# The first mixer's convolution by eight token phases with one fp32 product each, and the heads' query-key part emitted apart

## Chip, cores and metric

The kernel runs on one core of one Trainium2 chip. The metric is the device time of one execution in microseconds (us); the kernel before takes 2222.93 us (median of 3 runs, 2222.47 to 2223.78).

## The reference

A decoder trunk of two layers on x of 1024 tokens by 1024 channels, float32. Each layer is a mixer and a SwiGLU block (hidden width 2816), each with an RMS norm before it and a residual sum; a last RMS norm closes. The change is in the first layer's mixer, cut to what matters:

```python
ca, cg, q, k, v, og, gates = split(h @ w_in)       # 512 channels each, gates 8
u = ca * sigmoid(cg)
u = causal_depthwise_conv(u, conv_w, conv_b)       # 31 taps, 512 channels
u = silu(layernorm(u, ln_g, ln_b))                 # over the 512 channels
qk = silu(causal_depthwise_conv(concat(q, k), ...))  # 4 taps
hm = mlstm(q, k, v, gates)                         # 4 heads of 128
hm = head_rmsnorm(hm * sigmoid(og))
return concat(u, hm) @ w_out
```

The mLSTM works in chunks: scores of query and key with a decay, a state carried from chunk to chunk, and a stabiliser.

## The kernel before

Everything is kept channel by token, 128 channels on the partitions; tokens come in two halves of 512. Large products run in three passes (`mm3`, lines 142 to 144): every fp32 operand is split into a rounded part and the rest (a ScalarE copy and a VectorE subtraction: `split`, lines 126 and 127; for weights lines 137 and 138), and high times low, low times high and high times high are summed in PSUM. Weights come by a DMA (line 134) into one of two staging tiles `raw`, and their parts go to the tiles `wH` and `wL`, three buffers each. Small products (scores L513, transposes L517, state L536 to L539, means L348) are single fp32 products.

`mixer0` goes through the list `ORDER0`. `c` is `conv_in` for 128 channels: two projections, the gate, and a store of u by token phase to DRAM (L313, L316). `v` is `conv`, `l` the layer norm, `g` a head's value and output gate, `q` its query and key (`head_qk`), `x` its `head_mix` (a letter a or b after the number means one half), `n` a head norm, `k` the preparation of the output projection's right side (`cut`), which reads layer-norm tiles back (`conv_out`, L386) and finishes heads (`head_out`). The list gives the order of emission. A scheduler that simulates the program decides each engine's own order; `high_priority(offset)` pulls an instruction ahead.

The convolution folds the token axis into PH = 4 phases: a tile has 32 channels times 4 phases on the partitions, and NT = 256 steps of 4 tokens along the free axis. The 31 taps become SH + 1 = 9 band matrices of 128 by 128 (the first half empty), one for each shift. For each of 16 channel groups `conv` loads the bands (544 KB), splits them, loads the group's u from DRAM (L332), splits it to `uH` and `uL` (L126, L127), and runs 9 x 3 products of 256 columns into half a PSUM bank; ScalarE adds the bias on the way out (L339). `layer_norm` takes mean and variance with products by `ones_p` (L348), normalises, applies the affine and silu in 16 pairs of activations and a combine (L376 to L378), and stores by phase to `zd` (L380). `head_mix` first loads two rows (L507, L508), forms scores (L513) and transposed keys (L517), masks, takes exponentials (L519, L522), then runs the chunk products and the state (L536 to L558).

The output projection's weights come through the same tiles; for half 0 the fourth block of them uses the mixer's `u` tiles instead (`spare`, named `uw` in the trace).

Of the kernel before, what the change touches and what calls it, by code (L numbers as in the profile page):

```python
# [12 lines left out]
ALU = mybir.AluOpType  # L13
# [9 lines left out]
PH = 4  # L23
CG = 32
NT = T // PH
SH = 8
# [3 lines left out]
ORDER0 = ['c0', 'g0', 'c1', 'c2', 'q0', 'v0', 'c3', 'x0a', 'v1', 'x0b', 'g1', 'v2', 'q1', 'v3', 'x1', 'l', 'g2', 'q2', 'q3', 'x2a', 'g3', 'x3a', 'x2b', 'n3', 'k0', 'n1a', 'x3b', 'n1b']  # L30
CUT0 = (range(7), range(7, 8))
UB = 4
# [14 lines left out]
KB = 1  # L47
# [17 lines left out]
    0, 16, 32, 40, 56, 72, 88, 120, 128, 132, 136, 144)  # L65
# [3 lines left out]
def trunk_kernel(ctx, tc, xT, cols, gate_b0, ev_vo0, ev_u, ev_cw, ev_out, od_v0, od_u, od_out, gate_w2,  # L69
# [13 lines left out]
    def nm(s):  # L83
        uid[0] += 1
        return f"{s}_{uid[0]}"
# [23 lines left out]
    hln = cp.tile([P, 32], F32, tag="hln", name="hln")  # L109
    DVE.tensor_scalar(out=hln, in0=col[:, C_LG:C_LG + 32], scalar1=0.5, scalar2=None, op0=ALU.mult)  # L110
# [3 lines left out]
    def c1(i):  # L114
        return col[:, i:i + 1]
# [123 lines left out]
    def spare(src, mp):  # L239

        with tc.high_priority(offset=OOFF):
            raw = wp.tile([P, 1088], F32, tag="raw", name=nm("raw"), bufs=2)[:, :1024]
            SP.dma_start(raw, src)
            parts = []
            for c in range(2):
                hi, low = (mp.tile([P, HALF + 30], F32R, tag="u", name=nm("uw"), bufs=UB)[:, :HALF] for _ in range(2))
                split((hi, low), raw[:, c * HALF:(c + 1) * HALF], DVE)
                parts.append((hi, low))
        return parts


    def mixer0(cut, then):
        with tc.tile_pool(name="m0", bufs=1, reuse_waits="tile") as mp:
# [47 lines left out]
            def conv_in(i):  # L301

                wa = nextw(DVE)
                wg = nextw(DVE)
                for half in range(2):
                    u = mp.tile([P, HALF], F32, tag="u", name=nm("u"), bufs=UB)
# [6 lines left out]
                    DVE.scalar_tensor_tensor(out=u.rearrange("c (s n) -> c n s", s=PH), in0=g.rearrange("c (n s) -> c n s", s=PH),  # L313
                                             scalar=0.5, in1=rr[half].rearrange("c (n s) -> c n s", s=PH),
                                             op0=ALU.mult, op1=ALU.mult)
                    SP.dma_start(ud[i][:, :, half * P:(half + 1) * P], u.rearrange("c (s n) -> c s n", s=PH))  # L316

            def conv(i):


                for j in range(2):
                    b = bank("sm")
                    y = xy(2 * i + j if i < 2 else 2 * i + j - 4, int(i > 1))
                    Y.append(y)
                    for e in range(2):
                        g = 4 * i + 2 * j + e
                        w = weights(ev_cw[g], 1088, DVE)
                        c0 = (2 * j + e) * CG
                        with tc.high_priority(offset=WOFF):
                            raw = mp.tile([P, NT + SH], F32, tag="ur", name=nm("ur"), bufs=GB)  # L330
                            DVE.memset(raw[:, :SH], 0.0)
                            SP.dma_start(raw[:, SH:], ud[i][c0:c0 + CG].rearrange("c s n -> (c s) n"))  # L332
                            d = tuple(mp.tile([P, NT + SH], F32R, tag=t, name=nm(t), bufs=GB) for t in ("uH", "uL"))
# [9 lines left out]
            def by_phase(t):  # L343
                return t.rearrange("p (e n) -> p e n", e=2)

            def mean(b, s):
                for e in range(2):
                    PE.matmul(b, ones_p, s[:, e * NT:(e + 1) * NT], start=e == 0, stop=e == 1)  # L348

            def layer_norm():  # L350

                s = tp.tile([P, HALF], F32, tag="s", name=nm("s"), bufs=1)
                DVE.tensor_tensor(out=s, in0=Y[0], in1=Y[1], op=ALU.add)
                for y in Y[2:]:
                    DVE.tensor_tensor(out=s, in0=s, in1=y, op=ALU.add)
                mu = bank("sm")[:, :NT]
                mean(mu, s)
                s = tp.tile([P, HALF], F32, tag="s", name=nm("s"), bufs=1)
                for j, y in enumerate(Y):
                    DVE.tensor_tensor(out=by_phase(y), in0=by_phase(y), in1=mu.unsqueeze(1).to_broadcast([P, 2, NT]),  # L360
                                      op=ALU.subtract)
                    t = tmp() if j else s
                    ACT.activation(t, y, AF.Square)
                    if j:
                        DVE.tensor_tensor(out=s, in0=s, in1=t, op=ALU.add)
                var = bank("sm")[:, :NT]
                mean(var, s)
                r = tp.tile([P, HALF], F32, tag="r", name=nm("r"), bufs=1)[:, :NT]
                rsqrt(r, var)
                for j, y in enumerate(Y):  # L370
                    DVE.tensor_tensor(out=by_phase(y), in0=by_phase(y), in1=r.unsqueeze(1).to_broadcast([P, 2, NT]), op=ALU.mult)
                    t = tmp()
                    for e in range(2):
                        g = 2 * j + e
                        sl = slice(e * NT, (e + 1) * NT)
                        ACT.activation(t[:, sl], y[:, sl], AF.Tanh, bias=hln[:, 16 + g:17 + g], scale=hln[:, g:g + 1])  # L376
                        ACT.activation(y[:, sl], y[:, sl], AF.Identity, bias=hln[:, 16 + g:17 + g], scale=hln[:, g:g + 1])
                    DVE.scalar_tensor_tensor(out=y, in0=t, scalar=1.0, in1=y, op0=ALU.add, op1=ALU.mult)  # L378
                    for e in range(2):
                        SP.dma_start(zd[2 * j + e].rearrange("c a n -> a c n"), y[:, e * NT:(e + 1) * NT])  # L380

            def conv_out(k, half, d):

                z = xy(k, half)
                with tc.high_priority(offset=WOFF):
                    SP.dma_start(z.rearrange("c (a n) -> c a n", a=PH),  # L386
                                 zd[4 * k:4 * k + 4, :, :, half * P:(half + 1) * P].rearrange("g c a n -> (g c) a n"))
                z = z.rearrange("c (a n) -> c n a", a=PH)
                split(tuple(t.rearrange("c (n a) -> c n a", a=PH) for t in d), z, DVE)
# [113 lines left out]
            def head_mix(hd, half, q, k, v, og, st):  # L503
# [5 lines left out]
                cc, wk, em = gcols["c"], gcols["wk"], gcols["em"]  # L509
# [10 lines left out]
                for c in range(4):  # L520
# [7 lines left out]
                                  in1=wk[:, half * 4:half * 4 + 4, hd:hd + 1].to_broadcast([P, 4, P]), op=ALU.mult)  # L528
                for c2 in range(2):
# [57 lines left out]
            for what in ORDER0:  # L587
# [17 lines left out]
                elif what[0] == "x":  # L605
                    for half in halves:
                        heads[n]["s"] = head_mix(n, half, heads[n][0, half], heads[n][1, half], heads[n]["v"],
                                                 heads[n]["o"], heads[n]["s"] if half else None)
# [627 lines left out]
def _layout(i):  # L1236
# [22 lines left out]

    cw = i["ev_conv_w"][0].reshape(TAPS, 16, CG)  # L1260
    band = np.zeros((16, CG, PH, SH + 1, PH, CG), np.float32)
    for c in range(CG):
        for m in range(SH + 1):
            for sp in range(PH):
                for ap in range(PH):
                    j = 4 * (m - SH) + sp - ap + TAPS - 1
                    if 0 <= j < TAPS:
                        band[:, c, sp, m, ap, c] = cw[j, :, c]
    band = band.reshape(16, P, SH + 1, P)
    assert not band[:, :, 0, 64:].any()  # L1270
    band = cat([band[:, :, 1:].reshape(16, P, SH * P), band[:, :, 0, :64]], axis=2)
    qw = i["ev_qk_conv_w"][0].reshape(4, 8, P).transpose(2, 1, 0).reshape(P, 32)
    cols = cat([colv(i["mix_norm_g"]), colv(i["ffn_norm_g"]), colv(i["final_norm_g"]),
                phased(i["ev_conv_b"][0]), phased(i["ev_ln_g"][0]), phased(i["ev_ln_b"][0]), qw, colv(i["ev_qk_conv_b"]), colv(i["ev_head_g"]),
# [57 lines left out]
def _build(a):  # L1332
# [10 lines left out]
    args.append(nc.dram_tensor("zd", (16, CG, PH, NT), F32, kind="Internal").ap())  # L1343
# [15 lines left out]
```

## Time and profile before

| | before |
|---|---|
| median of 3 runs | 2222.93 us |
| profiled execution | 2222.86 us |
| its span, first to last instruction | 2221.1 us |
| TensorE products busy | 2181.1 us (98%) |
| VectorE busy | 1624.6 us (73%) |
| ScalarE busy | 899.2 us (40%) |
| mean granted TensorE clock | 0.995 |

The time of the execution is 1.8 us more than the span. TensorE's products are pipelined: a record's duration is longer than its distance to the next one, so what a product costs in a row of products is read from start to start. The granted clock is a share of 2.4 GHz; 0.5 is 1.2 GHz.

### The profile page before, as it was taken

The page shows a single profiled execution, that of the slowest core. Times are in us where ns is not written, and L with a number is a line of the kernel's source. Part 1 is how long each engine was busy: PE and PEld are TensorE (multiplying, and loading weights), DVE is VectorE, ACT ScalarE, POOL GpSimd, SP SyncE. Part 2 cuts the span into 40 slices and gives each one's busy share as a digit, 9 for nine tenths or more (in the row PEclk, how much of TensorE's full clock was granted, in tenths as well). Part 3 has the DMA queues.
Part 4 walks back from the last instruction along what each step waited for, and adds up shares of the span by engine and source line. Part 5 has one row for each costly group of instructions (what it writes and reads, how often), then busy time and mean ns, then how long its engine had stood idle before and what let it go on. Part 6 is the DMA issues. An engine that isn't in the chain of part 4 may idle for free.

```text
span 2221.1 us, 29368 instructions
## 1 busy us (share of the span) xinstructions
PE 2181.1 (98%) x10956; PEld 1851.6 (83%) x10956; DVE 1624.6 (73%) x2721; ACT 899.2 (40%) x1489; POOL 18.2 (1%) x56
## 2 busy tenths in 40 slices
PE   8999999899999999999999999999999999999997
PEld 6889899788888888888788989888788888888887
DVE  6564688669887677877867566677788877678686
ACT  5223364445222222444555444554432222234553
POOL 0000000000000000000020000000000000000000
PEclk9999999999999999999999999999999999999999
DMA  4233425536443324735421111044454423275343
GB/s 163 73 94 98 122 75 159 180 128 200 169 152 104 110 100 139 270 105 148 137 68 39 39 39 39 29 127 165 156 195 169 141 87 119 95 246 164 97 123 125
DMA packets 130719, 276.90 MB, mean 125 GB/s; under 512 B 13808, under 2 KB 31088, under 8 KB 130576
## 3 DMA queue, kind: packets, MB, share of 16 engines
q1 hardware_dynamic: 129424, 273.97, 37.9%
q8 instruction: 86, 1.41, 0.3%
q10 hardware_dynamic: 1152, 1.05, 0.1%
q14 instruction: 57, 0.47, 0.1%
HBM read 208.35 MB, written 66.62 MB: 124 GB/s over the span
## 4 chain that ended last, share of the span: by engine, by line
PE 92%; DVE 5%; ACT 1%; DMA 1%; issue 1%; DVEq 0%; SPq 0%; ACTq 0%
PE mm L142 20%; PE mm L143 20%; PE mm L144 20%; PE sm L142 9%; PE sm L143 9%; PE sm L144 9%; PE sm L775 1%; DVE xy L882 1%; PE sm L792 1%; PE sm L793 1%; PE sm L795 1%; DVE wL L138 0%; DVE xy L1227 0%; DMA raw<-in_ev_u 0%; DVE hL L127 0%
## 5 line engine op out<-in xcount | busy, mean ns | idle before, releaser
L143 PE MATMUL mm<-hL,wH 128*128 128x512 f32 x1420 | 558.0, 393 | 0.6 <-DVE hL L279 0.6
L144 PE MATMUL mm<-hH,wH 128*128 128x512 f32 x1420 | 557.4, 393 | 0.0
L142 PE MATMUL mm<-hH,wL 128*128 128x512 f32 x1420 | 525.5, 395 | 17.3 <-DVE wL L138 11.6
L142 PEld LDWEIGHTS mm<-hH,wL 128*128 128x128 f32 x1420 | 267.5, 189 | 74.9 <-ACT s L169 7.7
L143 PEld LDWEIGHTS mm<-hL,wH 128*128 128x128 f32 x1420 | 267.8, 189 | 57.0 <-DVE hL L279 2.1
L144 PEld LDWEIGHTS mm<-hH,wH 128*128 128x128 f32 x1420 | 267.8, 189 | 55.0
L143 PE MATMUL sm<-hL,wH 128*128 128x512 f32 x616 | 240.8, 391 | 0.0
L144 PE MATMUL sm<-hH,wH 128*128 128x512 f32 x616 | 239.9, 390 | 0.0
L142 PE MATMUL sm<-hH,wL 128*128 128x512 f32 x616 | 209.7, 391 | 0.6 <-DVE wL L127 0.5
L126 ACT ACTIVATE wH<-S 128x1024 fp32r<-128x1024 f32 x88 | 93.3, 1060 | 224.9 <-PE sm L144 223.2
L979 DVE TENSOR_TENSOR c<-sm,c 128x512 f32<-128x512 f32 x144 | 97.4, 689 | 113.4 <-PE sm L144 98.3
L126 ACT ACTIVATE wH<-q 128x512 fp32r<-128x512 f32 x143 | 90.4, 632 | 183.8 <-PE mm L144 104.3
L138 DVE TENSOR_TENSOR wL<-raw,wH 128x1024 fp32r<-128x1024 f32 (+2 forms) x95 | 117.5, 1236 | 61.1 <-ACT wH L137 61.0
L137 ACT ACTIVATE wH<-raw 128x1024 fp32r<-128x1024 f32 (+2 forms) x95 | 101.5, 1068 | 149.8 <-PE mm L144 96.3
L127 DVE TENSOR_TENSOR wL<-q,wH 128x512 fp32r<-128x512 f32 x143 | 98.9, 691 | 69.1 <-ACT wH L126 68.8
L142 PE MATMUL mm<-wH,hL 128*128 128x256 f32 (+2 forms) x512 | 144.5, 288 | 2.6 <-DVE t L310 1.9
L143 PE MATMUL mm<-wL,hH 128*128 128x256 f32 (+2 forms) x512 | 146.5, 288 | 0.0
L144 PE MATMUL mm<-wH,hH 128*128 128x256 f32 (+2 forms) x512 | 146.4, 288 | 0.0
L142 PEld LDWEIGHTS sm<-hH,wL 128*128 128x128 f32 x616 | 115.4, 188 | 25.6 <-DVE wL L127 0.7
L143 PEld LDWEIGHTS sm<-hL,wH 128*128 128x128 f32 x616 | 115.7, 188 | 25.3 <-issue 1.0
L126 ACT ACTIVATE wH<-raw 128x1024 fp32r<-128x1024 f32 x66 | 70.0, 1061 | 164.6 <-PE sm L144 130.4
L144 PEld LDWEIGHTS sm<-hH,wH 128*128 128x128 f32 x616 | 115.7, 188 | 24.3 <-issue 0.5
(302 smaller groups left out, 3941.0 us busy)
## 6 DMA issues: line engine op xcount, KB each, us to landing
raw<-in_w SPq DMA_DIRECT2D x108, 512.0 KB
mdT<-c SPq DMA_DIRECT2D x88, 256.0 KB
m<-mdT SPq DMA_DIRECT2D x88, 256.0 KB
mdB<-c SPq DMA_DIRECT2D x66, 256.0 KB
q<-in_w SPq DMA_DIRECT2D x60, 256.0 KB
m<-mdB SPq DMA_DIRECT2D x55, 256.0 KB
xsp<-xy SPq DMA_DIRECT2D x48, 256.0 KB
raw<-in_ev_u SPq DMA_DIRECT2D x22, 512.0 KB
```

What stands on the lines that cost most here:

```text
L126: ACT.activation(dst[0], src, AF.Copy)
L127: lo.tensor_tensor(out=dst[1], in0=src, in1=dst[0], op=ALU.subtract)
L137: ACT.activation(hi, raw, AF.Copy)
L138: lo.tensor_tensor(out=low, in0=raw, in1=hi, op=ALU.subtract)
L142: PE.matmul(o, lt[1], rt[0], start=start, stop=False)
L143: PE.matmul(o, lt[0], rt[1], start=False, stop=False)
L144: PE.matmul(o, lt[0], rt[0], start=False, stop=stop)
L775: PE.matmul(lb[:, j * P:(j + 1) * P], X[:, 2 * j * P:(2 * j + 1) * P], X[:, (2 * j + 1) * P:(2 * j + 2) * P], start=True, stop=True)
L792: PE.matmul(db[:, cc, :], kw[:, cs], v[:, c, :], start=True, stop=True)
L793: PE.matmul(ob[:, cc, :], A[:, cs], v[:, c, :], start=True, stop=st is None)
L795: PE.matmul(ob[:, cc, :], qt[:, cs], st, start=False, stop=True)
L979: DVE.tensor_tensor(out=out, in0=a, in1=b, op=ALU.add)
```

## The change

The convolution has 8 phases, 16 channels in a group, 32 groups, and 128 steps along the free axis; 5 full band matrices per group (320 KB), each with one fp32 product instead of three. Nothing is split: bands go by DMA into `wH` and `wL` in turn, data into one tile for four groups. The bias is added by VectorE for four groups at once. The affine and silu leave the layer norm for `conv_out`, behind the read from `zd`, where channels lie on the partitions. u is stored once for both halves. `head_mix` is cut in two, `head_pre` (row loads, scores, transposes, exponentials, scaled query and key) and the rest; `ORDER0` has `a` entries that emit `head_pre` earlier. The layout on the host and the constant columns follow.

```diff
-PH = 4
-CG = 32
-SH = 8
+PH = 8
+CG = 16
+SH = 4
-ORDER0 = ['c0', 'g0', 'c1', 'c2', 'q0', 'v0', 'c3', 'x0a', 'v1', 'x0b', 'g1', 'v2', 'q1', 'v3', 'x1', 'l', 'g2', 'q2', 'q3', 'x2a', 'g3', 'x3a', 'x2b', 'n3', 'k0', 'n1a', 'x3b', 'n1b']
+ORDER0 = ['c0', 'g0', 'c1', 'c2', 'q0', 'c3', 'a0a', 'v0', 'x0a', 'v1', 'x0b', 'g1', 'q1', 'a1a', 'v2', 'x1a', 'v3', 'x1b', 'l', 'g2', 'q2', 'a2a', 'q3', 'x2a', 'x2b', 'a3a', 'n3', 'g3', 'x3a', 'a3b', 'x3b', 'k0', 'n1a', 'n1b']
-UB = 4
+UB = 2
-KB = 1
+KB = 2
...
             def conv_in(i):
+                u = mp.tile([P, T], F32, tag="u", name=nm("u"), bufs=UB)
+                u4 = u.rearrange("c (s h n) -> c h n s", s=PH, h=2)
                 for half in range(2):
...
-                    SP.dma_start(ud[i][:, :, half * P:(half + 1) * P], u.rearrange("c (s n) -> c s n", s=PH))
+                SP.dma_start(ud[i], u)
...
             def conv(i):
...
-                    for e in range(2):
-                        g = 4 * i + 2 * j + e
-                        w = weights(ev_cw[g], 1088, DVE)
...
+                    with tc.high_priority(offset=WOFF):
+                        raw = mp.tile([P, 4, NT + SH], F32, tag="ur", name=nm("ur"), bufs=GB)
+                        DVE.memset(raw[:, :, :SH], 0.0)
+                        SP.dma_start(raw[:, :, SH:], ud[i][j * 64:(j + 1) * 64].rearrange("(g c) s n -> (c s) g n", g=4))
+                    for e in range(4):
+                        g = 8 * i + 4 * j + e
                         with tc.high_priority(offset=WOFF):
...
-                            split(d, raw, DVE)
+                            w = wp.tile([P, 1088], F32, tag="wL" if e % 2 else "wH", name=nm("cw"))[:, :(SH + 1) * P]
+                            SP.dma_start(w, ev_cw[g])
                         o = b[:, e * NT:(e + 1) * NT]
-                        for m in [1, 0] + list(range(2, SH + 1)):
-                            c, n = ((m - 1) * P, P) if m else (SH * P, P // 2)
-                            mm3(o[:n], tuple(t[:, c:c + n] for t in w), tuple(t[:, m:m + NT] for t in d), m == 1, m == SH)
-                        ACT.activation(y[:, e * NT:(e + 1) * NT], o, AF.Identity, bias=c1(C_CB + g), scale=1.0)
+                        for m in range(SH + 1):
+                            PE.matmul(o, w[:, m * P:(m + 1) * P], raw[:, e, m:m + NT], start=m == 0, stop=m == SH)
+                    g = 8 * i + 4 * j
+                    DVE.tensor_tensor(out=by_phase(y), in0=by_phase(b),
+                                      in1=col[:, C_CB + g:C_CB + g + 4].unsqueeze(2).to_broadcast([P, 4, NT]), op=ALU.add)
...
             def layer_norm():
...
-                    DVE.scalar_tensor_tensor(out=y, in0=t, scalar=1.0, in1=y, op0=ALU.add, op1=ALU.mult)
-                    for e in range(2):
-                        SP.dma_start(zd[2 * j + e].rearrange("c a n -> a c n"), y[:, e * NT:(e + 1) * NT])
+                    for e in range(4):
+                        SP.dma_start(zd[4 * j + e].rearrange("c a n -> a c n"), y[:, e * NT:(e + 1) * NT])
...
             def conv_out(k, half, d):
...
+                t = tmp()
+                ACT.activation(t, z, AF.Tanh, bias=hln[:, 4 + k:5 + k], scale=hln[:, k:k + 1])
+                ACT.activation(z, z, AF.Identity, bias=hln[:, 4 + k:5 + k], scale=hln[:, k:k + 1])
+                DVE.scalar_tensor_tensor(out=z, in0=t, scalar=1.0, in1=z, op0=ALU.add, op1=ALU.mult)
...
-            def head_mix(hd, half, q, k, v, og, st):
+            def head_pre(hd, half, q, k):
...
+                return q, rb, wb, kw
+
+            def head_mix(hd, half, pre, v, og, st):
+                q, rb, wb, kw = pre
```

## Rows read from the trace of the kernel before

**Rows 1.** The page: busy time of TensorE, and the chain that ended last by engine.

```profile
PE 2181.1 (98%) x10956; PEld 1851.6 (83%) x10956; DVE 1624.6 (73%) x2721; ACT 899.2 (40%) x1489; POOL 18.2 (1%) x56
...
PE 92%; DVE 5%; ACT 1%; DMA 1%; issue 1%; DVEq 0%; SPq 0%; ACTq 0%
```

**Rows 2.** The table by stretches (us from the span's start): busy time of each engine with its count of instructions, then granted clock, DMA share and GB/s.

```profile
134.00:157.00 23.00, 22.29 (x161) 20.67 (x160) 14.04 (x28) 8.54 (x18) 0.00 (x0) 1.00 0.39 125
157.00:181.00 24.00, 21.01 (x112) 17.94 (x110) 11.28 (x20) 6.62 (x14) 0.00 (x0) 0.99 0.37 107
...
222.00:232.00 10.00, 9.18 (x73) 8.59 (x72) 5.58 (x10) 4.44 (x8) 0.00 (x0) 1.00 0.62 188
...
260.00:276.00 16.00, 15.44 (x131) 15.19 (x130) 12.24 (x24) 7.99 (x17) 0.00 (x0) 1.00 0.44 134
...
312.00:330.00 18.00, 18.00 (x81) 14.89 (x80) 17.58 (x32) 16.79 (x31) 0.00 (x0) 1.00 0.22 67
...
400.00:425.00 25.00, 21.98 (x110) 18.23 (x110) 17.18 (x35) 8.19 (x22) 0.00 (x0) 0.93 0.56 193
...
181.00:190.00 9.00, 9.00 (x52) 9.00 (x53) 3.64 (x7) 1.87 (x6) 0.00 (x0) 0.66 0.36 102
```

**Rows 3.** TensorE's products in order of time (start, duration): the first of a channel group's 27, and the first behind the group.

```profile
153.26 0.28 PE L142 MATMUL sm<-uH,wL 128*128 128x256 f32 x1
...
156.49 0.39 PE L142 MATMUL mm<-hH,wL 128*128 128x512 f32 x1
```

**Rows 4.** Single fp32 products: the score product's records by its line, and pieces of the chain in order of time (start, length up to the next piece, records).

```profile
L513 PE MATMUL sm<-qk,qk x64: 270/275/422, 138.8 to 399.0; 128*128 128x128 f32 x64
...
138.99 0.89 PE sm L513 x8
...
146.61 0.24 PE sm L536 x2
...
289.09 0.86 PE sm L348 x4
```

**Rows 5.** Groups of instructions (busy us, mean ns of one, idle time of the engine before them and what ended it): the tap weights' two parts, a VectorE operation out of PSUM, and the first of the convolution's three products.

```profile
L137 ACT ACTIVATE wH<-raw 128x1088 fp32r<-128x1088 f32 x16 | 17.8, 1111 | 29.5 <-PE mm L144 16.3 <-PE sm L144 12.3 <-DMA raw<-in_ev_cw 0.8
...
L138 DVE TENSOR_TENSOR wL<-raw,wH 128x1088 fp32r<-128x1088 f32 x16 | 20.6, 1289 | 15.8 <-ACT wH L137 15.8
...
L360 DVE TENSOR_TENSOR xy<-xy,sm 128x512 f32<-128x512 f32 x8 | 4.9, 682 | 0.0
...
L142 PE MATMUL sm<-uH,wL 128*128 128x256 f32 x128 | 37.3, 291 | 4.6 <-ACT uH L126 4.1 <-DVE qk L496 0.5
```

**Rows 6.** TensorE in order of time: a convolution product, with the engine's idle time before it.

```profile
180.98 0.58 PE L142 MATMUL sm<-uH,wL 128*128 128x256 f32 x1 [2.99 <-ACT uH L126]
```

**Rows 7.** The chain that ended last, around that product.

```profile
174.61 3.97 DMA rb<-rowd
...
179.64 0.97 ACT rb L522 x3
180.61 0.32 ACT uH L126
...
184.12 0.21 PE sm L143
...
187.65 0.12 PE sm L143
```

**Rows 8.** The page: GB/s in 40 slices of 55.5 us, and the queue that carries nearly all transfers (packets, MB, share of 16 engines).

```profile
GB/s 163 73 94 98 122 75 159 180 128 200 169 152 104 110 100 139 270 105 148 137 68 39 39 39 39 29 127 165 156 195 169 141 87 119 95 246 164 97 123 125
...
q1 hardware_dynamic: 129424, 273.97, 37.9%
```

**Rows 9.** In order of time: the issue of a load of tap weights on SP's queue, and the copy that waited for it.

```profile
221.83 0.33 SPq L134 DMA_DIRECT2D raw<-in_ev_cw  x1
...
225.51 1.12 ACT L137 ACTIVATE wH<-raw 128x1088 fp32r<-128x1088 f32 x1 [0.75 <-DMA raw<-in_ev_cw]
```

**Rows 10.** Issues on SP's queue by tile (ns min/median/max, first and last start in us).

```profile
L316 SPq DMA_DIRECT2D ud<-u x8: 524/525/1330, 43.9 to 180.3; - x8
...
L380 SPq DMA_DIRECT2D zd<-xy x16: 508/528/740, 318.6 to 345.6; - x16
L386 SPq DMA_DIRECT2D xy<-zd x8: 547/568/617, 326.5 to 354.1; - x8
```

**Rows 11.** Groups of instructions up to 470 us: the layer norm's tanh and combine, a 512-wide activation, and table loads before the head norms.

```profile
L169 ACT ACTIVATE t<-xy 128x512 f32<-128x512 f32 x24 | 14.3, 619 | 2.7 <-DVE xy L232 1.7 <-DVE s L171 1.0
...
L376 ACT ACTIVATE t<-xy,hln 128x256 f32<-128x256 f32 x16 | 8.6, 587 | 0.0
...
L563 ACT ACT_TABLE_LOAD x2 | 2.6, 1283 | 0.0
...
L378 DVE SCALAR_TENSOR_TENSOR xy<-t,xy 128x512 f32<-128x512 f32 x8 | 5.5, 689 | 0.3 <-ACT xy L377 0.2
```

**Rows 12.** TensorE in order of time around the start of the output projection.

```profile
376.22 0.39 PE L142 MATMUL mm<-hH,wL 128*128 128x512 f32 x1
...
391.37 0.49 PE L536 MATMUL sm<-v,kw 128*128 128x129 f32 x2 [1.43 <-DVE kw L526]
...
396.26 0.96 PE L142 MATMUL mm<-hH,wL 128*128 128x512 f32 x3 [1.24 <-ACT den L550]
...
417.68 0.50 PE L142 MATMUL mm<-hH,wL 128*128 128x512 f32 x1 [2.80 <-DVE wL L138]
```

More of the change, by code (lines that the diff above doesn't have):

```diff
@@ L64 @@
 C_MIX, C_FFN, C_FIN, C_CB, C_LG, C_LB, C_QW, C_QB, C_HG0, C_GB, C_HG1, C_END = (
-    0, 16, 32, 40, 56, 72, 88, 120, 128, 132, 136, 144)
+    0, 16, 32, 40, 72, 76, 80, 112, 120, 124, 128, 136)
 @with_exitstack
@@ L106, in trunk_kernel @@
     SP.dma_start(gb0, gate_b0.partition_broadcast(P))
-    hln = cp.tile([P, 32], F32, tag="hln", name="hln")
-    DVE.tensor_scalar(out=hln, in0=col[:, C_LG:C_LG + 32], scalar1=0.5, scalar2=None, op0=ALU.mult)
+    hln = cp.tile([P, 8], F32, tag="hln", name="hln")
+    DVE.tensor_scalar(out=hln, in0=col[:, C_LG:C_LG + 8], scalar1=0.5, scalar2=None, op0=ALU.mult)
     hhg = cp.tile([P, 8], F32, tag="hhg", name="hhg")
@@ L243, in spare @@
             SP.dma_start(raw, src)
[L244 to L249, printed above, removed]
+            w = tuple(mp.tile([P, T], F32R, tag="u", name=nm("uw"), bufs=UB) for _ in range(2))
+            split(w, raw, DVE)
+        return w
     def mixer0(cut, then):
@@ L312, in conv_in @@
                     DVE.scalar_tensor_tensor(out=g, in0=g, scalar=1.0, in1=ba, op0=ALU.add, op1=ALU.mult)
-                    DVE.scalar_tensor_tensor(out=u.rearrange("c (s n) -> c n s", s=PH), in0=g.rearrange("c (n s) -> c n s", s=PH),
+                    DVE.scalar_tensor_tensor(out=u4[:, half], in0=g.rearrange("c (n s) -> c n s", s=PH),
                                              scalar=0.5, in1=rr[half].rearrange("c (n s) -> c n s", s=PH),
                                              op0=ALU.mult, op1=ALU.mult)
-                    SP.dma_start(ud[i][:, :, half * P:(half + 1) * P], u.rearrange("c (s n) -> c s n", s=PH))
+                SP.dma_start(ud[i], u)
             def conv(i):
@@ L324, in conv @@
                     Y.append(y)
-                    for e in range(2):
-                        g = 4 * i + 2 * j + e
-                        w = weights(ev_cw[g], 1088, DVE)
-                        c0 = (2 * j + e) * CG
-                        with tc.high_priority(offset=WOFF):
[L330 to L333, printed above, removed]
-                            split(d, raw, DVE)
-                        o = b[:, e * NT:(e + 1) * NT]
-                        for m in [1, 0] + list(range(2, SH + 1)):
-                            c, n = ((m - 1) * P, P) if m else (SH * P, P // 2)
-                            mm3(o[:n], tuple(t[:, c:c + n] for t in w), tuple(t[:, m:m + NT] for t in d), m == 1, m == SH)
-                        ACT.activation(y[:, e * NT:(e + 1) * NT], o, AF.Identity, bias=c1(C_CB + g), scale=1.0)
+                    with tc.high_priority(offset=WOFF):
+                        raw = mp.tile([P, 4, NT + SH], F32, tag="ur", name=nm("ur"), bufs=GB)
+                        DVE.memset(raw[:, :, :SH], 0.0)
+                        SP.dma_start(raw[:, :, SH:], ud[i][j * 64:(j + 1) * 64].rearrange("(g c) s n -> (c s) g n", g=4))
@@ L341, in mixer0 @@
+                    g = 8 * i + 4 * j
+                    DVE.tensor_tensor(out=by_phase(y), in0=by_phase(b),
+                                      in1=col[:, C_CB + g:C_CB + g + 4].unsqueeze(2).to_broadcast([P, 4, NT]), op=ALU.add)
             Y = []
             def by_phase(t):
-                return t.rearrange("p (e n) -> p e n", e=2)
+                return t.rearrange("p (e n) -> p e n", e=4)
             def mean(b, s):
-                for e in range(2):
-                    PE.matmul(b, ones_p, s[:, e * NT:(e + 1) * NT], start=e == 0, stop=e == 1)
+                for e in range(4):
+                    PE.matmul(b, ones_p, s[:, e * NT:(e + 1) * NT], start=e == 0, stop=e == 3)
@@ L359, in layer_norm @@
                 for j, y in enumerate(Y):
-                    DVE.tensor_tensor(out=by_phase(y), in0=by_phase(y), in1=mu.unsqueeze(1).to_broadcast([P, 2, NT]),
+                    DVE.tensor_tensor(out=by_phase(y), in0=by_phase(y), in1=mu.unsqueeze(1).to_broadcast([P, 4, NT]),
                                       op=ALU.subtract)
@@ L370, in layer_norm @@
                 for j, y in enumerate(Y):
[L371 to L377, printed above, removed]
-                    DVE.scalar_tensor_tensor(out=y, in0=t, scalar=1.0, in1=y, op0=ALU.add, op1=ALU.mult)
-                    for e in range(2):
-                        SP.dma_start(zd[2 * j + e].rearrange("c a n -> a c n"), y[:, e * NT:(e + 1) * NT])
+                    DVE.tensor_tensor(out=by_phase(y), in0=by_phase(y), in1=r.unsqueeze(1).to_broadcast([P, 4, NT]), op=ALU.mult)
+                    for e in range(4):
+                        SP.dma_start(zd[4 * j + e].rearrange("c a n -> a c n"), y[:, e * NT:(e + 1) * NT])
             def conv_out(k, half, d):
@@ L386, in conv_out @@
                     SP.dma_start(z.rearrange("c (a n) -> c a n", a=PH),
-                                 zd[4 * k:4 * k + 4, :, :, half * P:(half + 1) * P].rearrange("g c a n -> (g c) a n"))
+                                 zd[8 * k:8 * k + 8, :, :, half * 64:(half + 1) * 64].rearrange("g c a n -> (g c) a n"))
+                t = tmp()
+                ACT.activation(t, z, AF.Tanh, bias=hln[:, 4 + k:5 + k], scale=hln[:, k:k + 1])
+                ACT.activation(z, z, AF.Identity, bias=hln[:, 4 + k:5 + k], scale=hln[:, k:k + 1])
+                DVE.scalar_tensor_tensor(out=z, in0=t, scalar=1.0, in1=z, op0=ALU.add, op1=ALU.mult)
                 z = z.rearrange("c (a n) -> c n a", a=PH)
@@ L508, in head_mix @@
                 SP.dma_start(wb, rowd[1, hd, hs].partition_broadcast(P))
-                cc, wk, em = gcols["c"], gcols["wk"], gcols["em"]
+                cc, wk = gcols["c"], gcols["wk"]
                 sb = bank("sm")
@@ L528, in head_mix @@
                                   in1=wk[:, half * 4:half * 4 + 4, hd:hd + 1].to_broadcast([P, 4, P]), op=ALU.mult)
+                return q, rb, wb, kw
+            def head_mix(hd, half, pre, v, og, st):
+                q, rb, wb, kw = pre
+                em = gcols["em"]
                 for c2 in range(2):
@@ L606, in mixer0 @@
                     for half in halves:
-                        heads[n]["s"] = head_mix(n, half, heads[n][0, half], heads[n][1, half], heads[n]["v"],
-                                                 heads[n]["o"], heads[n]["s"] if half else None)
+                        pre = heads[n].get(("p", half)) or head_pre(n, half, heads[n][0, half], heads[n][1, half])
+                        heads[n]["s"] = head_mix(n, half, pre, heads[n]["v"], heads[n]["o"], heads[n]["s"] if half else None)
+                elif what[0] == "a":
+                    for half in halves:
+                        heads[n]["p", half] = head_pre(n, half, heads[n][0, half], heads[n][1, half])
                 elif what[0] == "n":
@@ L1256, in phased @@
         return np.tile(v.reshape(-1, CG).T, (PH, 1))
-    cw = i["ev_conv_w"][0].reshape(TAPS, 16, CG)
-    band = np.zeros((16, CG, PH, SH + 1, PH, CG), np.float32)
+    cw = i["ev_conv_w"][0].reshape(TAPS, 32, CG)
+    band = np.zeros((32, CG, PH, SH + 1, PH, CG), np.float32)
     for c in range(CG):
@@ L1265, in _layout @@
                 for ap in range(PH):
-                    j = 4 * (m - SH) + sp - ap + TAPS - 1
+                    j = PH * (m - SH) + sp - ap + TAPS - 1
                     if 0 <= j < TAPS:
                         band[:, c, sp, m, ap, c] = cw[j, :, c]
-    band = band.reshape(16, P, SH + 1, P)
-    assert not band[:, :, 0, 64:].any()
-    band = cat([band[:, :, 1:].reshape(16, P, SH * P), band[:, :, 0, :64]], axis=2)
+    band = band.reshape(32, P, (SH + 1) * P)
     qw = i["ev_qk_conv_w"][0].reshape(4, 8, P).transpose(2, 1, 0).reshape(P, 32)
     cols = cat([colv(i["mix_norm_g"]), colv(i["ffn_norm_g"]), colv(i["final_norm_g"]),
-                phased(i["ev_conv_b"][0]), phased(i["ev_ln_g"][0]), phased(i["ev_ln_b"][0]), qw, colv(i["ev_qk_conv_b"]), colv(i["ev_head_g"]),
+                phased(i["ev_conv_b"][0]), colv(i["ev_ln_g"][0]), colv(i["ev_ln_b"][0]), qw, colv(i["ev_qk_conv_b"]), colv(i["ev_head_g"]),
                 colv(i["od_gate_b"]), colv(i["od_head_g"])], axis=1)
@@ L1342, in _build @@
     args.append([nc.dram_tensor(f"ud_{k}", (P, PH, NT), F32, kind="Internal").ap() for k in range(4)])
-    args.append(nc.dram_tensor("zd", (16, CG, PH, NT), F32, kind="Internal").ap())
+    args.append(nc.dram_tensor("zd", (32, CG, PH, NT), F32, kind="Internal").ap())
     args.append(nc.dram_tensor("ad", (LEAD, 2, P, HALF), F32, kind="Internal").ap())
```

1 line of the change is left out of this document (removed).

## Prediction

> **What bounds the kernel now.** I read the page's busy times and its chain that ended last, then a table by stretches, then single instructions where the change works. TensorE is busy in 98% of the span and holds 92% of the chain; VectorE holds 5%, DMA 1% [rows 1]. So time comes from TensorE's work and from its idle moments; work elsewhere counts only where TensorE ends up waiting for it. The convolution lies between 134 and 276 us. In the stretches of it that are shown [rows 2] TensorE falls short of full by 0.7, 3.0, 0.8 and 0.6 us, and VectorE is busy for 14 of 23, 11 of 24, 6 of 10 and 12 of 16 us. From 312 to 330 us, in the layer norm, VectorE is busy in 17.6 of 18 us while TensorE stays full: there another engine is near its limit. Durations come from one execution of 2222.86 us, of which 2221.1 are the span; the median of the runs shown is 2222.93, so the sum is made against 2222.9.
>
> **The change, part by part.**
>
> *Products.* Before, a channel group is 9 shifts times 3 products of 256 columns. In an undisturbed group the first of the 27 starts at 153.26 and the next instruction at 156.49: 3.23 us, 0.12 each [rows 3]. Sixteen such groups are 51.7 us; I count 51.2, since some products stand 0.117 apart. After, there are 32 groups of 5 fp32 products of 128 columns, 160 in all. The nearest row is the heads' score product L513: fp32, 128x128 weights of its own, 128 columns. It leaves two records for each product (64 for 32), and four products (x8) fill 0.89 us up to the next instruction [rows 4]: 0.2225 each. Two more rows bound it: two 256-column fp32 products of L348 (x4) take 0.86, so 0.215 per 128 columns, and one of L536, 129 columns, takes 0.24. That is 34.4 to 38.4 us; I take L513, of equal form: 160 x 0.2225 = 35.6. **Term 1: -15.6** (-12.8 to -16.8). All of it is on the path, since TensorE is full. The layer norm's means stay: 8 products of 128 columns (1.78) for 4 of 256 (1.72).
>
> *Splits.* Gone are 16 ScalarE copies and 16 VectorE subtractions of the tap weights (17.8 and 20.6 us), the same pair for the data tiles, and 16 bias activations; 8 additions out of PSUM come in, 0.68 each by L360 [rows 5]. Neither engine is the bound here, so this alone is worth nothing. But TensorE waited 4.1 us in all for ScalarE's copy of the data [rows 5], 2.99 of them at 180.98 [rows 6]. That one is a queue: a row load for a head takes 3.97 us from 174.61, VectorE's mask and ScalarE's exponentials L522 follow, and behind these on ScalarE stood the copy [rows 7]. Afterwards the convolution's operands come from a DMA alone, and 4.1 us go. The long wait also took the clock down: from 181 to 190 us the granted clock is 0.66, so 1.2 GHz for two thirds of it [rows 2], and a product follows its neighbour by 0.21 instead of 0.12 [rows 7]; 9 x 0.34 = 3.1 us. **Term 2: -7.2** (0 to -7.2; 0 if other waits take their place). The 0.5 at 134 to 157 for a head's operand stays.
>
> *Weight stream.* Tap weights grow from 16 x 544 KB to 32 x 320 KB, 8.9 to 10.5 MB. They go straight into the six slots of wH and wL (three each) instead of two staging buffers; with 2.1 MB of data tiles it is 12.6 MB. Back to back, a group takes 5 x 0.2225 = 1.11 us, and the queue would have to bring 12.6 MB in 35.6 us, 354 GB/s. The trace gives its limit by an estimate: 273.97 MB at 37.9% of 16 engines over 2221 us is 325 GB/s if never idle; the fullest slice of the page moved 270 [rows 8], the fullest stretch of the convolution 188 [rows 2]. At 325 it is 38.7 us: 3.1 of waiting. Latency alone makes no wait: a slot comes up again six groups (6.7 us) later, and the longer load of before was issued at 221.83 and used at 225.51 [rows 9]. Bounds: 0, if heads' work lies between the groups, and 31.3 at 188. I take 325, as the slower rows were demand and no limit. **Term 3: +3.1.** The Trainium skill (DMA: Bandwidth & Descriptors, Specifications) gives a core about 358 GB/s of HBM; by that estimate there is no wait and the sum is 3.1 lower. No row here shows that rate.
>
> *SP's queue.* A tap-weight load now waits for a slot that TensorE frees, where it waited for VectorE. Behind it on SP stand data loads, heads' row loads and the next projection's weights, which now have both staging buffers to themselves. SP issues 16 more weight loads (0.33 each [rows 9]), 8 fewer data loads, which with four blocks each should cost what the store of u does (0.53), 4 fewer stores of u, and 16 more layer-norm stores (0.53) [rows 10]: some 11 us more, spread over 260. The store of u moves behind both halves; its other 256 KB are 0.8 us at 325, hidden by the next projections. Zero; if the cover were gone, 1.11 us, one group, for each wait.
>
> *Late silu.* Affine and silu move from 16 pairs of 256-wide activations ahead of the store (0.587 each) to 8 pairs of 512-wide ones behind the load (0.619 by L169): ScalarE saves 18.8 - 9.9 = 8.9 us, and 5.5 us of VectorE (L378) leave the stretch where it is full [rows 11]. Against it, tanh now lands among the heads' square roots and exponentials, where changing the table costs 1.28 us [rows 11], and at 391 to 418 us TensorE already waits 1.43, 1.24 and 2.80 [rows 12]. I take two more table loads on the path. **Term 4: +2.6** (0 to 5.1). The layer-norm stores, 32 x 0.53 = 17 us on SP, are slower than what feeds them, but the last gather was issued at 354.1 [rows 10] and the output projection's products start at about 376 [rows 12].
>
> *Order.* The query-key part moves ahead: the same instructions, its two row loads earlier, a second kw buffer. Beyond term 2 I take nothing, between -5.5 (the three waits at 391 to 418 gone) and +2.8 (one more like the longest).
>
> Sum: 2222.9 - 15.6 - 7.2 + 3.1 + 2.6 = **2205.8**, say 2206.
>
> **Rivals.**
> *Late give-back.* Four gathered tiles of half 0 must pass tanh, affine and combine (0.619 + 0.619 + 0.69) before their split; on the path ahead of the output projection that is 4 x 1.93 = 7.7, and with two more table loads (2.6) 2216. For: TensorE's waits at 391 to 418 [rows 12]. Against: the gathers ended 20 us early. The Trainium skill (DMA: Bandwidth & Descriptors, Specifications) also asks for 512 B or more for the full rate; the gather's runs fall from 512 to 256 B. No row shows such runs; the rule would speak for this rival.
> *The weight stream decides: slower.* If the convolution's loads come at the 188 GB/s of its best stretch [rows 2], 12.6 MB take 66.9 us against 35.6: 31.3 of waiting, 2222.9 - 22.8 + 31.3 = 2231. It decides from 216 GB/s down (12.6 MB in 35.6 + 22.8 us). For: the new order puts eight groups, half a head and eight groups in a row, with no projection between. Against: 270 GB/s in the slice of 888 to 944 us [rows 8].
> *More than forecast.* No wait for weights, no table loads, and the late order also removes the 5.5 us of waits and the clock behind them, 25 x 0.07 = 1.8 [rows 2, 12]: 2193.
>
> **How the numbers follow.** Forecast, 2198 to 2213: 0.58. Late give-back, to 2218: 0.16. More than forecast: 0.08. Weight stream: 0.11. The remaining 0.07 is gain and loss within 0.2%, 4.4 us, about what a measurement of this kernel can tell. So faster 0.82, same 0.07, slower 0.11. The range, 2193 to 2219, leaves out the stream, and the tails.
>
> **What would show it.** Right: the convolution as 320 records about 0.111 apart, 35.6 us in all; no wait for ScalarE before them; a granted clock near 1.00 where 181 to 190 had 0.66; the output projection's first products some 20 us earlier. Term 3 is wrong if TensorE's idle time before these products is far from 3 us; term 4 if its idle time before the output projection for ScalarE and VectorE does not grow by about 3. The whole is wrong if an accumulating fp32 product takes over 0.32 us (51.2 / 160), or if idle time grows by as much as the products shrink.

## The result, and the profile after

The changed kernel takes 2193.21 us (median of 4 runs, 2192.64 to 2195.03) against 2223.3 on the same chip: ratio 0.9868, interval 0.9856 to 0.9881, some 29 us less. The forecast was 2206, 17 us less, in a range of 2193 to 2219; the time lies at its lower end, 0.2 us inside, where the rival *more than forecast* stood, and two of the four runs lie below 2193. The profiled execution took 2195.03 us, its span 2193.3. Of the runs below one, of e7 (2410.25 us at a mean granted clock of 0.848), is left out of its ratio.

Busy times and the chain by engine, which answer to [rows 1]:

```profile
PE 2161.4 (99%) x10852; PEld 1832.3 (84%) x10852; DVE 1603.7 (73%) x2688; ACT 866.4 (40%) x1424; POOL 18.2 (1%) x56
...
PE 92%; DVE 5%; ACT 1%; issue 1%; DMA 1%; DVEq 0%; SPq 0%; ACTq 0%
```

TensorE fills 99% of a shorter span; VectorE and ScalarE are busy for 21 and 33 us less. The stretches, with the columns of [rows 2]:

```profile
157.00:181.00 24.00, 23.78 (x211) 23.44 (x210) 12.27 (x30) 5.42 (x17) 0.00 (x0) 1.00 0.74 243
240.00:256.00 16.00, 15.78 (x139) 15.59 (x138) 10.57 (x23) 5.86 (x17) 0.00 (x0) 1.00 0.65 194
345.00:400.00 55.00, 52.88 (x316) 46.15 (x315) 45.56 (x91) 34.93 (x79) 0.00 (x0) 1.00 0.56 181
1060.00:1075.00 15.00, 12.85 (x50) 10.15 (x50) 12.96 (x22) 6.87 (x13) 0.00 (x0) 0.89 0.45 158
```

The first two hold the convolution: TensorE is short by 0.2 us each, the clock is at 2.4 GHz, and the queue moves up to 243 GB/s. The third holds the output projection's start, with no lower clock where [rows 2] had 0.93. The last row is new: far behind the change the clock is at 1.2 GHz for part of 15 us, where the kernel before had 1.00 in the same work (1085 to 1110), and 15 x 0.11 = 1.65 us of the 29.5 gained up to the first SwiGLU block are given back. Why the clock falls there was not settled; e3 below, with the same convolution, has 1.00 from 1000 to 1100 us, the changed kernel 0.98.

A block of two bank fills (eight groups, 40 products, 80 records) in the chain that ended last, answering to [rows 3, 4], and what the chain goes by while the second block runs:

```profile
157.60 8.93 PE sm L334 x80
...
169.29 5.74 DMA rb<-rowd
```

What TensorE waited for between 44 and 470 us (total us, times, longest), before:

```profile
PE sm L142 <- ACT uH L126: 4.1, 3, 3.0
PE mm L142 <- DVE wL L138: 3.3, 3, 2.8
PE sm L536 <- DVE kw L526: 1.4, 1, 1.4
PE mm L142 <- ACT den L550: 1.2, 1, 1.2
PE sm L142 <- DVE qk L496: 0.5, 1, 0.5
PE sm L539 <- DVE st L545: 0.2, 1, 0.2
```

and after (kw is a head's scaled key, st its state, wL the low part of a weight):

```profile
PE sm L537 <- DVE kw L522: 1.2, 2, 0.8
PE sm L537 <- DVE st L543: 0.7, 1, 0.7
PE sm L540 <- DVE st L546: 0.7, 3, 0.2
PE mm L142 <- DVE wL L138: 0.4, 1, 0.4
```

The line of one of the two moved activations (ns min/median/max), and the queue's line of [rows 8]:

```profile
L381 ACT ACTIVATE xy<-xy,hln x8: 799/804/962, 334.2 to 348.9; 128x512 f32<-128x512 f32 x8
...
q1 hardware_dynamic: 136336, 275.54, 38.9%
```

80 records in 8.93 us are 0.1116 each, 320 are 35.7. No wait for a tap load is in the list, none for ScalarE; 3.0 us of waits are left of 10.7. The output projection's first product starts at 355.63; before it was 374.74, a little ahead of the first row of [rows 12].

Added up, each from its start to the next product's start, all that stands at the convolution's records falls from 59.7 to 35.7 us, waits and lower clock within it included: 24.0. Up to the first SwiGLU block the kernel gains 29.5. The other 5.5 lie at the heads and the output projection's start.

### The profile page after: what moved, and what is told of

Its sections match the earlier page's. It is cut to its first block, busy times and chain, and to the rows that moved or that the text cites. A ratio compares the mean times of both kernels' runs of the same rounds, so it can differ in the third digit from the quotient of the medians.

```text
span 2193.3 us, 29046 instructions
## 1 busy us (share of the span) xinstructions
PE 2161.4 (99%) x10852; PEld 1832.3 (84%) x10852; DVE 1603.7 (73%) x2688; ACT 866.4 (40%) x1424; POOL 18.2 (1%) x56
## 4 chain that ended last, share of the span: by engine, by line
PE 92%; DVE 5%; ACT 1%; issue 1%; DMA 1%; DVEq 0%; SPq 0%; ACTq 0%
PE mm L142 20%; PE mm L143 20%; PE mm L144 20%; PE sm L142 8%; PE sm L143 8%; PE sm L144 8%; PE sm L334 1%; PE sm L779 1%; DVE hL L127 1%; DVE xy L886 1%; PE sm L796 1%; PE sm L797 1%; PE sm L799 1%; DVE xy L1231 0%; DVE wL L138 0%
## 5 line engine op out<-in xcount | busy, mean ns | idle before, releaser
L137 ACT ACTIVATE wH<-raw 128x1024 fp32r<-128x1024 f32 (+2 forms) x79 | 83.7, 1059 | 127.2 <-PE mm L144 93.4
L138 DVE TENSOR_TENSOR wL<-raw,wH 128x1024 fp32r<-128x1024 f32 (+2 forms) x79 | 96.7, 1224 | 49.3 <-ACT wH L137 49.3
```

What stands on the lines that cost most here:

```text
L137: ACT.activation(hi, raw, AF.Copy)
L138: lo.tensor_tensor(out=low, in0=raw, in1=hi, op=ALU.subtract)
```

## The experiments

Each kernel's ratio is to the kernel before, run beside it; the changed kernel's is 0.9868 (0.9856 to 0.9881). 0.001 is 2.2 us.

**The new convolution in the old order** (e1).

```diff
 (the changed kernel)
+ORDER0 = [... the list of the kernel before ...]
```

> The changed kernel with the order list of the kernel before, so every query-key part is emitted where its head is mixed. Theory: some 24 of the 30 us come from the convolution itself (59.7 us of TensorE's time from start to start before, 35.7 after) and some 6 from the late order, so 2198 to 2201, with waits of TensorE of 1 us and more back around the start of the output projection. Rival (the convolution gives it all, the order nothing): 2192 to 2195. Second rival (the weight stream binds once the order puts nothing between the groups, or the reverse): idle time before the tap products.

Measured: 2206.16, ratio 0.9932 (0.9920 to 0.9945). Some 15 us, half the gain, less than the theory gave. TensorE's waits (cw is a load of tap weights), and the stretch of the output projection's start:

```profile
PE sm L537 <- DVE kw L522: 6.0, 3, 2.4
PE mm L142 <- DVE wL L138: 3.3, 2, 2.8
PE sm L540 <- DVE st L546: 1.0, 3, 0.5
PE sm L334 <- DMA cw<-in_ev_cw: 0.3, 1, 0.3
```

```profile
350.00:410.00 60.00, 51.50 (x266) 44.02 (x265) 43.41 (x88) 30.87 (x74) 0.00 (x0) 0.89 0.48 156
```

The products are as cheap as after the whole change (36.5 us), but 8.5 us of waits and a clock of 0.89 over 60 us take back some 7 more than in the kernel before. The rival that the order gives nothing is out, and so is a binding weight stream (0.3 us).

**The old convolution in the new order** (e2): the query-key part cut off, two kw buffers.

```diff
 (the kernel before)
+KB = 2
+ORDER0 = [... the new list ...]
+def head_pre(hd, half, q, k): ...
```

> The kernel before with the query-key part cut off, the new order list and two kw buffers; the convolution stays in three passes over parts. Theory: the late waits go (about 6 us) and the convolution's 59.7 us stay, so 2215 to 2218. Rival (the order gives nothing by itself): 2222 to 2224. Second rival (with no projections between the tap groups the splits on ScalarE and VectorE come too late): 2226 to 2240.

Measured: 2218.83, ratio 0.9987 (0.9978 to 0.9996). About 3 us, below the theory's 6; the runs spread from 2215.72 to 2221.53. The late waits do go, but of the convolution's waits for the splits 2.8 us stay (uH), and one of 2.9 for a tap weight's low part is new, as the second rival had it in kind:

```profile
PE sm L142 <- DVE wL L138: 2.9, 1, 2.9
PE sm L142 <- ACT uH L126: 2.8, 3, 1.7
```

So 15 + 3 do not make 29: the order is worth far more beside the fast convolution.

**No early query-key parts at all** (e3), **none behind the layer norm** (f1).

```diff
-'c3', 'a0a', 'v0', ... 'q1', 'a1a', 'v2', ... 'q2', 'a2a', 'q3', 'x2a', 'x2b', 'a3a', 'n3', 'g3', 'x3a', 'a3b', 'x3b', ...
+e3: every a entry taken out;  f1: a2a, a3a, a3b taken out
```

> The changed kernel without the entries that emit the query-key part early; all else in its order. Theory: what helped the order is that the last heads are mixed before the output projection is prepared, not the early part, so 2193 to 2196. Rival (the early part takes the waits away): 2198 to 2201, with waits of TensorE for kw or the state back.

> The changed kernel without the three early query-key parts behind the layer norm (heads 2 and 3); the front keeps its two. Without all five the kernel took 2206.3. Theory: a head's mix is a chain from TensorE over VectorE back to TensorE that needs other work of TensorE beside it, and the faster convolution leaves less of that everywhere; the tail's three carry about half of the loss, the front's two the rest: 2198 to 2202. Rival (the tail alone, just ahead of the output projection): 2204 to 2208. Second rival (the front alone): 2193 to 2195.

Measured: e3 2206.29, ratio 0.9933 (0.9921 to 0.9946); f1 2199.48, ratio 0.9900 (0.9883 to 0.9916). The theory for e3 failed: the early part does matter, some 14 us by the ratios, more than its rival had. About half of it falls to the tail (f1) and half to the front, as expected for f1. TensorE's waits in e3, and two of its stretches:

```profile
PE sm L537 <- DVE kw L522: 5.4, 3, 2.0
PE sm L540 <- DVE st L546: 2.0, 4, 0.8
PE sm L537 <- DVE st L543: 1.4, 1, 1.4
PE sm L537 <- DVE st L546: 1.1, 1, 1.1
```

```profile
160.00:176.00 16.00, 14.00 (x109) 13.47 (x108) 6.03 (x16) 1.04 (x6) 0.00 (x0) 0.89 0.75 251
350.00:390.00 40.00, 33.08 (x220) 28.99 (x220) 33.30 (x78) 25.88 (x68) 0.00 (x0) 1.00 0.38 113
```

A head's mix is a chain: transposes on TensorE, kw on VectorE, state products on TensorE. Emitted in one piece it leaves TensorE idle, in the tail for 6.9 of 40 us, and in the front the clock falls with the waits. e3 and f1 keep the second kw buffer; whether the early parts need it was not tried.

**The old tail behind the layer norm** (e6), **the last half head late** (f2).

```diff
+e6: ... 'l', 'g2', 'q2', 'q3', 'x2a', 'g3', 'x3a', 'x2b', 'n3', 'k0', 'n1a', 'x3b', 'n1b'
+f2: ... 'x3a', 'a3b', 'k0', 'n1a', 'x3b', 'n1b'
```

> The changed kernel with the order list of the kernel before from the layer norm on: the front keeps its early query-key parts, heads 2 and 3 lose theirs and the last head is mixed beside the output projection again. Theory: the tail costs 6 to 9 us (kw and state waits around the start of the output projection and a lower clock behind them): 2199 to 2203. Rival (the front's early parts carry it): 2193 to 2196.

> The changed kernel with the second half of the last head mixed behind the preparation of the output projection, as the kernel before has it, all else as changed. Theory: the old tail's cost (2204.9 with early parts gone and this order) is mostly here, the 2.8 us wait for a weight and the lower clock behind it come back: 2198 to 2203. Rival (the place of the last mix does not matter once its query-key part is early): 2193 to 2195.

Measured: e6 2204.88, ratio 0.9916 (0.9904 to 0.9929); f2 2196.71, ratio 0.9891 (0.9877 to 0.9906). The tail costs 11 us when all of it is undone, more than expected: e6 has 8.3 us of waits from 134 to 410 us and a clock of 0.92 from 345 to 400. f2 lies between its two expectations, and its interval touches that of the changed kernel; its trace has the expected wait back (2.54 us for wL at 390.69), and the clock is 0.95 over 34 us:

```profile
376.00:410.00 34.00, 30.29 (x143) 24.77 (x142) 18.62 (x33) 13.31 (x27) 0.00 (x0) 0.95 0.58 194
```

So the last head's place seems to be a part of it (5 us by the ratio), and the early parts (f1, 7 us) the larger.

**Silu back in the layer norm** (e7): by phase, so 64 activations of 128 columns.

```diff
 (layer_norm)
+for e in range(4):
+    ACT.activation(t[:, sl], y[:, sl], AF.Tanh, ...)
+    ACT.activation(y[:, sl], y[:, sl], AF.Identity, ...)
+DVE.scalar_tensor_tensor(out=y, in0=t, scalar=1.0, in1=y, op0=ALU.add, op1=ALU.mult)
 (conv_out)
-... the same on z, 512 columns wide ...
```

> The changed kernel with affine and silu back in the layer norm, by phase, in 32 pairs of 128-wide activations ahead of the store. Theory: their place matters little, since TensorE waits for neither: 2193 to 2197. If the fourth term was right (late silu costs 2.6 us): 2190 to 2191. Rival (VectorE and ScalarE are at their limit in the layer norm's stretch and the extra activations push them past it): 2198 to 2210.

Measured: 2205.66, ratio 0.9920 (0.9907 to 0.9932), 11 to 12 us worse than the change: the rival. One wait of TensorE tells it, first in the list of waits, then in the chain:

```profile
PE mm L142 <- DVE wL L138: 8.8, 2, 8.4
```

```profile
310.96 1.15 ACT xy L375 x3
312.11 0.95 ACT wH L137
...
313.09 1.24 DVE wL L138
...
314.37 0.79 PE mm L142
```

From 295.8 to 312 ScalarE runs these activations (0.48 each) without a break, and a projection's weight split (L137) stands behind them on the same engine; from 296 to 320 the clock is 0.79. With eight phases, the late silu is what keeps the weights coming. The version changes the place and the number of the activations together (64 for 16); the two were not taken apart.

**Padded tap loads** (e5): 544 KB for 320.

```diff
 (conv)
-w = wp.tile([P, 1088], F32, tag="wL" if e % 2 else "wH", name=nm("cw"))[:, :(SH + 1) * P]
+w = wp.tile([P, 1088], F32, tag="wL" if e % 2 else "wH", name=nm("cw"))
 (host)
 band = band.reshape(32, P, (SH + 1) * P)
+band = cat([band, np.zeros((32, P, 1088 - (SH + 1) * P), np.float32)], axis=2)
```

> The changed kernel with each tap load padded from 320 to 544 KB (17.8 MB for 10.5), the padding unused. If the third term was right and the queue's 325 GB/s bind while groups run back to back, four blocks of eight groups need 19.9 MB / 325 = 61 us against 36: TensorE waits some 25 us on the tap loads, 2215 to 2220. Theory after the trace (which shows no wait for tap loads): the loads run ahead while projections and heads lie between the blocks, so 2193 to 2200, with a few short waits at most.

Measured: 2196.66, ratio 0.9883 (0.9870 to 0.9896), just above the change, with overlapping intervals. In its first stretch the queue is busy for 0.98 of the time, and TensorE is short by only 1.9 and 1.6 us:

```profile
157.00:181.00 24.00, 22.11 (x189) 21.31 (x188) 13.53 (x31) 5.02 (x16) 0.00 (x0) 1.00 0.98 358
240.00:256.00 16.00, 14.36 (x125) 14.01 (x124) 9.22 (x21) 6.08 (x17) 0.00 (x0) 1.00 0.89 318
```

The longest of its waits between 134 and 277 us is not for the tap loads (0.2 in all) but for the convolution's data, tile ur:

```profile
PE sm L334 <- DMA ur<-ud: 1.5, 2, 1.2
```

70% more bytes of taps cost some 3 us (the convolution's records fill 38.3 us for 35.7). The third term was wrong: the changed kernel's 243 GB/s have room below 358.

**Four phases, one product** (e4); **eight phases, three passes** (e8).

```diff
 (e4: the kernel before)
-w = weights(ev_cw[g], 1088, DVE)
+SP.dma_start(w, ev_cw[g])
...
-split(d, raw, DVE)
-mm3(o[:n], tuple(t[:, c:c + n] for t in w), tuple(t[:, m:m + NT] for t in d), m == 1, m == SH)
+PE.matmul(o[:n], w[:, c:c + n], raw[:, m:m + NT], start=m == 1, stop=m == SH)
 (e8: the changed kernel)
-SP.dma_start(w, ev_cw[g])
+w = weights(ev_cw[g], (SH + 1) * P, DVE)
...
+split(d, raw, DVE)
-PE.matmul(o, w[:, m * P:(m + 1) * P], raw[:, e, m:m + NT], start=m == 0, stop=m == SH)
+mm3(o, tuple(t[:, m * P:(m + 1) * P] for t in w), tuple(t[:, e, m:m + NT] for t in d), m == 0, m == SH)
```

> The kernel before with one fp32 product in place of three passes, and no splits, but still four phases: 9 products of 256 columns for each of 16 groups. Theory: a 256-column fp32 product costs 0.43 us by the means' row, 16 x 9 x 0.43 = 61.9 against 51.2 of products, while the waits for ScalarE's copy and the clock behind them (7.2) go: 2225 to 2228, so it is the eight phases that pay. Rival (dropping the splits is what pays, whatever the phases): 2205 to 2215.

> The changed kernel with eight phases and three passes over parts: 32 groups of 5 shifts times 3 products of 128 columns, 480, with the splits of taps and data back. If a pass of 128 columns costs half of one of 256 (0.06 us), products fall to 29 us from 36, and only the splits can take that back: 2186 to 2200. If it costs as much as a 128-column fp32 record (0.11), products are 53 us and the phases alone give nothing over the kernel before: 2205 to 2215.

Measured: e4 2243.82, ratio 1.0100 (1.0086 to 1.0114); e8 2242.43, ratio 1.0092 (1.0075 to 1.0109). Neither half alone pays; both lose 20 us, more than expected. In e4 a group fills 4.23 us of the chain, 16 of them 67.7; 0.47 for a product, not 0.43. e4 has the old order, so its fair neighbour is e1, which has eight phases and all else of the change but the order: e4 takes 38 us more, 31 of them at the convolution's records (67.9 us against 36.5). In e8 two neighbours stand 0.11 apart at the full clock, hardly less than the 0.12 with 256 columns [rows 3], and for long stretches twice that; its records take 84.0 us, against 53 by the second expectation. Of the rest some 23 us are the lower clock (226 records stand 0.215 apart) and some 6 the waits, nearly all for the splits:

```profile
200.64 4.23 PE sm L338 x18
```

```profile
160.16 0.28 PE L143 MATMUL sm<-uL,wH 128*128 128x128 f32 x1
160.27 0.28 PE L144 MATMUL sm<-uH,wH 128*128 128x128 f32 x1
```

```profile
180.00:200.00 20.00, 19.27 (x91) 19.08 (x90) 9.89 (x21) 7.26 (x20) 0.00 (x0) 0.50 0.42 122
```

**Half the columns** (f4): three of five tap products stream 64 columns, and that part of the convolution is left out.

```diff
+n = NT if m in (0, SH) else NT // 2
-PE.matmul(o, w[:, m * P:(m + 1) * P], raw[:, e, m:m + NT], start=m == 0, stop=m == SH)
+PE.matmul(o[:, :n], w[:, m * P:(m + 1) * P], raw[:, e, m:m + n], start=m == 0, stop=m == SH)
```

> The changed kernel with three of each group's five tap products reduced to 64 of their 128 columns; that part of the convolution is left out. 96 of 160 products are concerned, 192 records of 0.111. If a record's cost follows its columns, they fall to 0.056 and the kernel to about 2182. Rival (loading 128 columns of weights sets a record's cost, whatever it streams): no change, 2191 to 2195, and then sixteen phases of 64 columns could not beat eight.

Measured: 2193.16, ratio 0.9874 (0.9859 to 0.9889): no change, the rival. The block takes what it took with all columns:

```profile
156.15 8.93 PE sm L335 x80
```

A record costs 0.11 us with 64 or 128 fp32 columns, so up to 128 columns what sets it is not what it streams (with 256 columns it is 0.216, e4). Its 128 columns of weights are the same in both, but that they set it was not tried by itself.

**All query-key parts early** (f3).

```diff
+'a0a', 'v0', 'a0b', 'x0a', ... 'a1a', 'v2', 'a1b', 'x1a', ... 'a2a', 'a2b', 'q3', 'x2a', 'x2b', 'a3a', 'n3', 'g3', 'a3b', 'x3a', ...
```

> The changed kernel with the query-key part of every half emitted ahead of the mix before it. Theory: what is left of TensorE's waits for kw and the state in the first mixer (some 3 us) goes: 2190 to 2193. Rival (two row buffers and two kw buffers let nothing run further ahead, and the rest waits for the state, not for kw): 2193 to 2195.

Measured: 2198.79, ratio 0.9901 (0.9886 to 0.9916): slower than the change by 0.003 in the ratio, some 7 us, against both theories. Its list of waits is longer by 2.5 us (1.7 for rb, a head's row tile, is new). That is most of the 3.5 us between the two profiled executions (2198.48 and 2195.03), but not of the 7 by the ratio; the rest stays open. No version tried beats the changed kernel.

## Why the prediction was right, and where its sizes were off

*Products.* Right: 320 records 0.1116 apart, 35.7 us (forecast 35.6). That all of it is on the path was not quite so: 240 of the records lie in the chain that ended last, and while the second 80 run (169 to 178 us) it goes by the load of a head's row tile (5.74 us from 169.29) and the work behind it, so a still shorter convolution may run into that, which was not tried. f4 adds that the row L513 was the right one to take: a 128-column record is at its floor.

*Splits.* Right: the three waits for ScalarE's copy and the lower clock at 181 to 190 are gone; terms 1 and 2 together said 22.8, the records show 24.0. But in e1 the faster convolution without the order gains only 15 us: the waits for kw at the heads grow from 1.4 to 6.0, and the clock falls. The bound "0 if other waits take their place" was the real case without the early parts.

*Weight stream.* Wrong by +3.1: no wait. The limit that I worked out, 325 GB/s, is a mean over all transfers, and not all of them move as much for their time on the queue. After the change it is busy for 0.96 of a stretch in which nearly all packets are the 256 B of the layer norm's gathers, and moves 207 GB/s:

```profile
314.00:318.00 4.00, 4.00 (x20) 3.30 (x19) 3.67 (x7) 0.44 (x2) 0.00 (x0) 1.00 0.96 207
```

In e5, with long rows, it moves 358 at a share of 0.98. The Trainium skill (DMA: Bandwidth & Descriptors, Specifications) gives about 358 GB/s of HBM for a core: e5's row agrees, and the sum by it was the better one. Eight groups run without pause (80 records in 8.93 us), the next eight start within 3 us of them, and neither waits for a tap load.

*Late silu.* Wrong: forecast +2.6, and the moved activations cost nothing that can be seen. The two table loads that were its reason did not come: up to 450 us ScalarE loads a table 11 times in either profile, in the whole execution 40 times. An activation takes 0.80 us and not 0.619, but TensorE waits for none. Keeping them early, with eight phases, costs 11 to 12 us (e7): I costed the table loads on ScalarE, and missed what stands behind the activations on that engine, the next projection's weight split. That the affine by phase would be 64 narrow activations with eight phases I had not worked out either; the 16 pairs of before were no measure for it.

*Order.* I took nothing and gave -5.5 as the end. The three waits at 391 to 418 [rows 12] did go, with the clock behind them, 7.3 as the rival had it; but 2.6 us of waits for kw and the state are there now, and what the records show outside the convolution is 5.5. Between the profiled executions the spans differ by 27.8 us, 10.7 more than the forecast's 17.1: 1.2 at the convolution's records, 5.7 of terms 3 and 4 that did not come, 5.5 here, less the 1.65 given back. So the mechanism of terms 1 and 2 carried the gain; that the range held, by 0.2 us, owes something to luck, since term 4 was wrong, term 3 went by too low a limit, and the order was left at nothing.

*Rivals.* Late give-back and the weight stream did not come. (The 2216 of late give-back adds two table loads to the two that the 2205.8 already held.) The gathers' slow runs of 256 B kept nothing waiting: they were issued by 319.4, and the products that use them start at 355.63. What the sum could not show is that its parts are not independent: the order alone gives 3 us (e2), all but the order 15 (e1), together 29; leave out the early parts (e3), the tail (e6) or the late silu (e7) and 11 to 14 us are gone each time. Each removal brings waits for other things (kw and state, a weight, a split behind activations), and mostly a lower clock behind them; that is shown. Why the removals cost about the same was not tried.

## What to carry to other kernels

When a change shortens work that fills TensorE while a chain of other engines runs beside it, look for the chains that it covered, and emit their first parts earlier; here the gain with the shorter work alone was half of what both gave. Cost a moved step by what stands behind it on its engine, not by its own length. Before splitting an fp32 product into passes, count records: here one fp32 product of 128 columns is two records, three passes are three, each at 0.11.

## What the runs showed of the hardware that was not expected

- A record's distance to the next did not fall below 0.11 us, with 64 fp32 columns (f4), 128 fp32 columns (after) or 128 columns of a pass (e8). So sixteen phases of 64 columns, 64 groups of 3 products (384 records, about 43 us by 0.1116), should not beat eight: an estimate, not run.
- In e8 the granted clock fell to 1.2 GHz behind a wait of 1.18 us at 165.74 and was 0.50 from 180 to 200 us although TensorE was busy for 19.27 of 20 us; the same groups as fp32 records after the change kept 1.00. What in these passes keeps the clock down was not settled.
- In e4 the change from 128 to 64 columns of weights within a group cost extra: the two records of the 64-column product, the one before and the one behind take 0.27 to 0.32 us to the next start instead of 0.216, some 0.34 us a group (read from 200.7 to 201.9 us).
